# q, k, v and gates in three parts with borders by column group, sigmoid by tanh, and modulation work moved around the first attention

## The chip, the cores and the metric

The kernel runs on one core of one Trainium2 chip. The metric is the device time of one execution in microseconds, the median of several runs. TensorE (PE) multiplies, with its weight loads (PEld) beside it; VectorE (DVE), ScalarE (ACT) and GpSimd (POOL) do the rest; SyncE's queue (SP) issues all transfers.

## What is computed

A trunk of two layers over 256 tokens of width 2048, all in float32. Cut to what matters here:

```python
c_act = silu(c)
for l in range(2):
    mod = c_act @ ada_w[l] + ada_b[l]                   # 6 x 2048
    sh_a, sc_a, gt_a, sh_m, sc_m, gt_m = split(mod, 6)
    h = rmsnorm(x, norm_mix[l]) * (1 + sc_a) + sh_a
    qa, ka, va, qb, kb, vb, ga, gb = split_cols(h @ w_in[l])
    ya = window_attention(rotary(rmsnorm(qa)), rotary(rmsnorm(ka)), va, sink) @ w_proj_a[l]
    yb = neighbourhood_attention(rmsnorm(qb), rmsnorm(kb), vb, bias) @ w_proj_b[l]
    x = x + gt_a * ((sigmoid(ga) * ya + sigmoid(gb) * yb) @ w_out[l])
    h = rmsnorm(x, norm_ffn[l]) * (1 + sc_m) + sh_m
    g, v = split(depthwise_conv(h @ w_up[l]), 2)
    x = x + gt_m * ((silu(g) * v) @ w_down[l])
```

## The kernel before

**Weights.** The host lays all weight matrices out as a stream of 128x128 blocks in the order in which they are used (`block_stream`). A *unit* is 16 blocks, 1 MiB, one transfer (`w<-in_ws`, L255) into one of the four buffers of the pool `raw`. ACT casts each half of a unit to a rounded high part (L264), DVE subtracts it from the weight for the low part (L265); both lie in one of the four buffers `hl`. PE multiplies with three products (high by high, low by high, high by low). `features` has weights as the stationary side and 256 tokens as the moving one, 3 matmuls of 256 columns a block (L273 to L275). `tokens`, used for q, k, v, has the activations stationary and four blocks, 512 columns, moving (L331 to L333), for two halves of the tokens. A unit is 48 matmuls of 256 columns or 24 of 512. A layer is 232 units.

**Modulation.** `ada` makes `mod` in 96 steps a layer: each loads 1 MiB (`aw<-in_aw`, L195) into a buffer of the same pool `raw`, and one DVE instruction (L196) multiplies it by silu(c) and sums it. Steps 0 to 31 of layer 0 give shift and scale of the first norm; `ada_and_h` makes chunk kc of the modulated input h (16 chunks of 128 features; `normed`, L403 on DVE, L406 on ACT, L407 on DVE) after its two steps.

**Order of the work.** Each time the stream has used up a unit, `tick` runs: background jobs in `Paced` advance by their rate (steps per unit), and `plan(l, u)` makes modulation steps until their number lies on the line between the corners (unit, steps) of `ADA_PLAN_0` or `ADA_PLAN_1`. In layer 0 the job that makes h has the rate `FIRST_RATE`. From this the framework places each instruction in its engine's queue, which runs in order.

**Layer 0, stage by stage (unit numbers are those of the stream).** The input projection runs over the 2048 inputs in four parts of 2, 4, 5 and 5 chunks of h (`K_PARTS_0`), so that it can begin before h is complete. In each part come nine groups of 512 columns of q, k, v (`QKV_GROUPS`) and 16 chunks of gate A; a part begins when all its chunks of h are in the program. The borders lie at units 6.5, 19.5 and 35.75, the end at 52. In the first part ACT copies the sums out (L751, L787); in the later ones DVE adds them to what is there (L753, L782). In the last part `qk_rows` normalises q and k (L483 to L509; the power of -0.5 on POOL, L378) and turns them on PE (L516). The job `attention` starts after the third group of the last part with rate `ATT`, one new head at most a step, eight heads A and then eight heads B: scores (L528), row maximum (L532), exp (L540), scaling by the reciprocal (L548), transposes (L553), product with v (L559), between the matmuls of the stream. Gate A gets its sigmoid in the last part (L785). Then come the projection of A times its gate (L796, units 52 to 60), gate B with its sigmoid (L810, units 60 to 76), the projection of B times gate B plus ya, split into high and low (L822 to L824), the output projection and the feed-forward network.

**Layer 1** has its h complete before the projection, which is one part there; eight gate chunks are made first from the not yet normalised input (`bare_gate`, L663).

```python
for pi, part in enumerate(parts):
    if l == 0 and pi > 0:
        while done[0] < 2 * (part[-1] + 1):
            next(job0)
    last = pi == len(parts) - 1
    for g in range(len(QKV_GROUPS)):
        pss = st.tokens(h, part)
```

Of the kernel before, what the change touches and what calls it, by code (L numbers as in the profile page):

```python
# [9 lines left out]
F32 = mybir.dt.float32  # L10
F32R = mybir.dt.float32r
AF = mybir.ActivationFunctionType
ALU = mybir.AluOpType
AX = mybir.AxisListType

P = 128
L = 2
D = 2048
S = 256
KC = D // P  # L20
# [12 lines left out]
QKV_GROUPS = [1024, 0, 512, 2560, 3584, 1536, 3072, 4096, 2048]  # L33
GATE_A, GATE_B = 4608, 6656
# [2 lines left out]
FF_GROUPS = [list(range(sum(FF_SIZES[:i]), sum(FF_SIZES[: i + 1]))) for i in range(3)]  # L37


K_PARTS_0 = [2, 4, 5, 5]  # L40
K_PARTS = [[range(sum(K_PARTS_0[:i]), sum(K_PARTS_0[: i + 1])) for i in range(len(K_PARTS_0))], [range(KC)]]

FIRST_TURN = 3
OUT_TURNS = [range(0, FIRST_TURN)] + [[mo] for mo in range(FIRST_TURN, KC)]

ADA_PLAN_0 = [(38, 32), (58, 48), (76, 66), (84, 70), (98, 80), (108, 80), (231, 143)]
ADA_PLAN_1 = [(8, 143), (76, 166), (84, 168), (99, 176), (108, 176), (128, 184), (142, 192)]

FIRST_RATE = 0.65
ENDING = 15  # L50
FIRST = 0

# [18 lines left out]
def block_stream(l):  # L71

    seq = []
    bare = BARE[0] if l else 0
    if l:
        for kc in range(KC):
            seq += [("w_in", kc, GATE_A // P + mo) for mo in range(SIDE)]
        for mo in range(SIDE, bare):
            seq += [("w_in", kc, GATE_A // P + mo) for kc in range(KC)]
    for part in K_PARTS[l]:  # L80
        for g in QKV_GROUPS:
            for kc in part:
                seq += [("w_in", kc, g // P + j) for j in range(4)]
        for mo in range(bare, KC):
            seq += [("w_in", kc, GATE_A // P + mo) for kc in part]
    for mo in range(KC):
        seq += [("w_proj_a", kc, mo) for kc in range(HA)]
    for mo in range(KC):
        seq += [("w_in", kc, GATE_B // P + mo) for kc in range(KC)]
    for mo in range(KC):  # L90
        seq += [("w_proj_b", kc, mo) for kc in range(HB)]
    for mos in OUT_TURNS:
        seq += [("w_out", kc, mo) for kc in range(KC) for mo in mos]
    for gi, chunks in enumerate(FF_GROUPS):
        cols = [c + h * FC for c in chunks for h in range(2)]
        if gi == 0:
            for kc in range(KC):
                seq += [("w_up", kc, m) for m in cols[:SIDE]]
            cols = cols[SIDE:]
        for m in cols:  # L100
            seq += [("w_up", kc, m) for kc in range(KC)]
        for mos in OUT_TURNS:
            seq += [("w_down", kc, mo) for kc in chunks for mo in mos]
    return seq
# [11 lines left out]
def encoder(ctx: ExitStack, tc: tile.TileContext, a: dict, out: bass.AP):  # L116
    nc = tc.nc
# [14 lines left out]
    at = pool("at", 2)  # L132
# [40 lines left out]
    def led(name):  # L173

        t = hp.tile([P, KC * 2 * S + OFF], F32R, name=name, tag="h")
        at = [0] + [OFF + 2 * S * k for k in range(1, KC)]
        return [t[:, i : i + 2 * S].rearrange("p (a s) -> p a s", a=2) for i in at]
# [6 lines left out]
    mods, amods, nrms, done = {}, {}, {}, {0: 0, 1: 0}  # L184
# [63 lines left out]
    bg = Paced()  # L248
# [86 lines left out]
                    self.tick()  # L335
            return pss

    def split(dst, src):
        nc.scalar.copy(dst[:, 0], src)
        nc.vector.tensor_tensor(out=dst[:, 1], in0=src, in1=dst[:, 0].bitcast(F32), op=ALU.subtract)  # L340

    def warm(n):

# [73 lines left out]
    class Bare:  # L417
# [47 lines left out]
        def at(self):  # L465
            return {SQUARES_AT: self.squares, ROOTS_AT: self.roots}

        def level(self, ps):

            z = ev.tile([P, S], F32, name="lev", tag="z")  # L470
            sh = sm.tile([P, 3], F32, name="lsh", tag="lsh")
            nc.scalar.activation(out=sh[:, 1:], in_=ps[:, S : S + 2], func=AF.Copy, accum_out=sh[:, :1])
            nc.vector.tensor_tensor(out=z[:], in0=ps[:, :S], in1=self.rbs[:], op=ALU.mult)
            return z, sh

# [103 lines left out]
    def plan(l, u):  # L579

        corners = (ADA_PLAN_0, ADA_PLAN_1)[l]
        for (u0, n0), (u1, n1) in zip(corners, corners[1:]):
# [33 lines left out]
    ps = ax.tile([P, 2], F32, name="ss_in", tag="ss", bufs=1)  # L616
# [28 lines left out]
    for l in range(L):  # L645
        st = Stream(l) if l == 0 else nxt
        mod = mods.get(l)
        if l == 0:
            h = led("h0_0")
            job0 = ada_and_h(first_h(h))  # L650
            while done[0] < 2 * len(K_PARTS[0][0]):
                next(job0)
            mod = mods[0]
            bg.add(job0, FIRST_RATE)

        ya = place("o", 16, F32, f"ya{l}")
        if l:


            def bare_gate(mo):  # L660
                def evac(ps):
                    z, sh = bare.level(ps)
                    nc.scalar.activation(out=ya[:, mo], in_=z[:], func=AF.Sigmoid, bias=sh[:, :1])  # L663

                return evac

            st.features(bare.chunks, [bare_gate(mo) for mo in range(SIDE)], at=bare.at())
            for mo in range(SIDE, BARE[0]):
                st.features(bare.chunks, [bare_gate(mo)])
            bg.finish(bare.steps)  # L670
            h = bare.h
# [61 lines left out]
                next(job)  # L733

        hs = h
        parts = K_PARTS[l]
        for pi, part in enumerate(parts):
            if l == 0 and pi > 0:
                while done[0] < 2 * (part[-1] + 1):
                    next(job0)  # L740
            last = pi == len(parts) - 1
            for g in range(len(QKV_GROUPS)):
                pss = st.tokens(h, part)
                if pi == 0 and g == 0:
                    gains, sink, cw, rots = small(l)
                dst = packs[g // 3][:, 4 * (g % 3) : 4 * (g % 3) + 4]
                rows = dst.rearrange("p (t a) s -> p t (a s)", t=2)
                if not last or pi > 0:
                    for t, ps in enumerate(pss):
                        if pi == 0:  # L750
                            nc.scalar.copy(rows[:, t], ps[:])  # L751
                        else:
                            nc.vector.tensor_tensor(out=rows[:, t], in0=ps[:], in1=rows[:, t], op=ALU.add)  # L753
                    pss = [rows[:, t] for t in range(2)]
                if not last:
                    continue

                def have(g=g):
                    ready[0] = g + 1

                vcol = {0: GA * HEAD, 4: 0, 7: 0}.get(g)
                if vcol is not None and pi == 0:
                    for t in range(2):
                        nc.scalar.copy(rows[:, t, vcol:], pss[t][:, vcol:])
                if g == 0:
                    qk_rows(pss, GA, rots[1], gains[:, 1:2], kTa, have)
                elif g < 3:
                    qk_rows(pss, 4, rots[0], gains[:, 0:1], dst, have)
                elif vcol is None:
                    qk_rows(pss, 4, None, gains[:, 3:4] if g in (3, 6) else gains[:, 2:3], dst, have)  # L770
                else:
                    have()
                if g == 2:
                    bg.add(job, ATT[l])


            for mo in range(BARE[0] if l else 0, KC):

                def gate_a(ps):
                    src = ps  # L780
                    if pi > 0:
                        nc.vector.tensor_tensor(out=ya[:, mo], in0=ps, in1=ya[:, mo], op=ALU.add)  # L782
                        src = ya[:, mo]
                    if last:
                        nc.scalar.activation(out=ya[:, mo], in_=src, func=AF.Sigmoid)  # L785
                    elif pi == 0:
                        nc.scalar.copy(ya[:, mo], ps)  # L787

                st.features([hs[k] for k in part], [gate_a])


        attended(HA)
        for mo in range(KC):

            def proj_a(ps):
                nc.vector.tensor_tensor(out=ya[:, mo], in0=ps, in1=ya[:, mo], op=ALU.mult)  # L796

            st.features(oA, [proj_a])
        bg.pace(job, ATT_B[l])
        gb = []  # L800
# [6 lines left out]

        def gate_b(mo):
            def evac(ps):
                nc.scalar.activation(out=gb[mo], in_=ps, func=AF.Sigmoid)  # L810

            return evac

# [3 lines left out]
        merged = led(f"merged{l}")  # L817
        for mo in range(KC):

            def merge(ps):  # L820
                z = ev.tile([P, S], F32, name="m", tag="z")
                nc.vector.tensor_tensor(out=z[:], in0=ps, in1=gb[mo], op=ALU.mult)  # L822
                nc.vector.tensor_tensor(out=z[:], in0=z[:], in1=ya[:, mo], op=ALU.add)
                split(merged[mo], z[:])  # L824

            st.features(oB, [merge])

# [6 lines left out]
        bare = Bare(l, 1, sums)  # L834
# [27 lines left out]
        for gi, chunks in enumerate(FF_GROUPS):  # L862
# [34 lines left out]
            for cs in sets:  # L897
                fns = [lambda p, e=e, c=c: e(p, c) for c in cs for e in (g_evac, v_evac)]
                src = bare.chunks if gi == 0 and cs[0] < BARE[1] // 2 else bare.h
# [36 lines left out]
        if l < L - 1:  # L936
            bare = over
# [75 lines left out]
```

## Time and profile before

| | |
|---|---|
| Time, median of 3 runs | 2703.92 us (2703.27 to 2705.94) |
| The profiled execution | 2704.2 us, span 2702.4 us, granted clock 0.996 |
| PE busy | 2660.9 us, 98% of the span |
| DVE busy | 2099.4 us, 78% |
| ACT busy | 1411.0 us, 52% |
| Transfers | 700.38 MB, mean 259 GB/s |
| DVE, weights' low parts (L265) | 928 of 1222 ns |
| DVE, modulation steps (L196) | 192 of 2348 ns |
| ACT, weights' high parts (L264) | 928 of 1049 ns |
| ACT, table loads | 29 of 1283 ns |

The profile is of one execution. A busy PE need not run at its pace: matmuls are pipelined and a late one counts as busy for longer, so the number of matmuls in a stretch says more than the share. Durations of neighbours on DVE and ACT overlap by some 0.09 us: a duration is the mean of one instruction, and the chain of waits shows what each adds.

### The profile page before, as it was taken

To read this page: it belongs to the slowest core of one execution; us is meant where nothing else is said; L and a number is where in the kernel's file an instruction comes from. 1 tells how busy PE (TensorE), PEld (TensorE's weight loads), DVE (VectorE), ACT (ScalarE), POOL (GpSimd) and SP (SyncE) were. 2 spreads that over 40 slices of the span, in tenths; PEclk is the share of its full clock that TensorE was granted. 3 is DMA by queue.
4 is the path that set the end of the run, shared out by engine and by line. 5 is a ranking of instruction groups with operands and counts; after the bars stand their busy time and mean duration, and the time that the engine had idled before them with its cause. 6 is when DMAs were issued, how large, how long until landed. Compare 5 with 4: busy or idle time off the path is not lost.

```text
span 2702.4 us, 50217 instructions
## 1 busy us (share of the span) xinstructions
PE 2660.9 (98%) x21088; PEld 2565.8 (95%) x21088; DVE 2099.4 (78%) x2941; ACT 1411.0 (52%) x2081; POOL 35.1 (1%) x24
## 2 busy tenths in 40 slices
PE   7899999999999999999999999999999999999999
PEld 5688799999999999999998889999999999999999
DVE  6998987897987888788886666658879866655664
ACT  5344684455754455345564556544565445543553
POOL 0000100000000000000000000000000000000000
PEclk9899999999999999999999999999999999999999
DMA  8887578987688888878766656666757775555554
GB/s 319 329 340 272 218 288 313 356 309 265 235 296 297 291 293 286 296 290 297 291 217 250 241 209 231 233 237 254 292 184 283 285 265 197 188 200 190 190 200 142
DMA packets 101892, 700.38 MB, mean 259 GB/s; under 512 B 12705, under 2 KB 15009, under 8 KB 17697
## 3 DMA queue, kind: packets, MB, share of 16 engines
q1 hardware_dynamic: 101666, 697.17, 70.7%
q8 instruction: 165, 2.70, 0.4%
q14 instruction: 61, 0.50, 0.0%
HBM read 695.03 MB, written 2.10 MB: 258 GB/s over the span
## 4 chain that ended last, share of the span: by engine, by line
PE 91%; DVE 4%; DMA 1%; ACT 1%; POOL 1%; issue 1%; SPq 0%; POOLq 0%; ACTq 0%; DVEq 0%
PE ps L273 26%; PE ps L275 25%; PE ps L274 25%; PE ps_t L332 4%; PE ps_t L333 4%; PE ps_t L331 4%; DVE aw L196 1%; DVE hl L265 1%; PE po L559 1%; PE sc L528 1%; DMA aw<-in_aw 1%; POOL qrs L378 1%; PE tp L553 0%; ACT hl L264 0%; DVE qn L492 0%
## 5 line engine op out<-in xcount | busy, mean ns | idle before, releaser
L265 DVE TENSOR_TENSOR hl<-w,hl 128x1024 fp32r<-128x1024 f32 x928 | 1130.2, 1222 | 362.5 <-ACT hl L264 360.9
L264 ACT CAST hl<-w 128x1024 fp32r<-128x1024 f32 x928 | 971.1, 1049 | 771.9 <-PE ps L275 487.1
L273 PE MATMUL ps<-h,hl 128*128 128x256 f32 x3328 | 925.1, 278 | 0.0
L275 PE MATMUL ps<-h,hl 128*128 128x256 f32 x3328 | 923.6, 278 | 0.9 <-DVE hl L265 0.9
L274 PE MATMUL ps<-h,hl 128*128 128x256 f32 x3328 | 921.9, 277 | 0.0
L275 PEld LDWEIGHTS ps<-h,hl 128*128 128x128 f32 x3328 | 625.4, 188 | 1.5 <-DVE hl L265 1.3
L273 PEld LDWEIGHTS ps<-h,hl 128*128 128x128 f32 x3328 | 625.9, 188 | 0.5
L274 PEld LDWEIGHTS ps<-h,hl 128*128 128x128 f32 x3328 | 625.3, 188 | 0.4
L196 DVE CUSTOM_DVE_ANT_0 aw<-aw,cact,ab 128x2048 f32<-128x2048 f32 x192 | 450.8, 2348 | 62.8 <-DMA aw<-in_aw 62.0
L331 PE MATMUL ps_t<-hl,h 128*128 128x512 f32 x576 | 227.4, 399 | 7.9 <-ACT hl L264 7.3
L332 PE MATMUL ps_t<-hl,h 128*128 128x512 f32 x576 | 228.4, 397 | 5.2 <-DVE hl L265 5.2
L333 PE MATMUL ps_t<-hl,h 128*128 128x512 f32 x576 | 228.1, 396 | 0.9 <-DVE h L407 0.9
L858 DVE SCALAR_TENSOR_TENSOR u<-ps,cw,u 128x255 f32<-128x255 f32 x304 | 146.2, 481 | 68.0 <-ACT u L856 64.0
L856 ACT ACTIVATE u<-ps,cw 128x256 f32<-128x256 f32 x152 | 85.7, 564 | 185.6 <-PE ps L275 185.4
L275 PE MATMUL ps<-merged,hl 128*128 128x256 f32 x512 | 142.1, 278 | 0.0
L274 PE MATMUL ps<-merged,hl 128*128 128x256 f32 x512 | 141.8, 277 | 0.0
L273 PE MATMUL ps<-merged,hl 128*128 128x256 f32 x512 | 141.8, 278 | 0.0
L274 PE MATMUL ps<-act_o,hl 128*128 128x256 f32 x512 | 141.6, 277 | 0.0
L275 PE MATMUL ps<-act_o,hl 128*128 128x256 f32 x512 | 141.6, 276 | 0.0
L273 PE MATMUL ps<-act_o,hl 128*128 128x256 f32 x512 | 141.4, 277 | 0.0
L331 PEld LDWEIGHTS ps_t<-hl,h 128*128 128x128 f32 x576 | 109.5, 190 | 31.9 <-ACT hl L264 8.4
L332 PEld LDWEIGHTS ps_t<-hl,h 128*128 128x128 f32 x576 | 109.8, 191 | 30.9 <-DVE hl L265 8.2
(209 smaller groups left out, 4574.1 us busy)
## 6 DMA issues: line engine op xcount, KB each, us to landing
w<-in_ws SPq DMA_DIRECT2D x464, 1024.0 KB, 4.9
aw<-in_aw SPq DMA_DIRECT2D x192, 1024.0 KB, 5.7
bias<-in_bias SPq DMA_DIRECT2D x16, 256.0 KB, 4.5
x<-in_xT SPq DMA_DIRECT2D x4, 512.0 KB, 5.4
out<-x SPq DMA_DIRECT2D x16, 128.0 KB, 2.3
cw<-in_cw SPq DMA_DIRECT2D x2, 176.0 KB, 4.5
maskA<-in_maskA SPq DMA_DIRECT2D x1, 256.0 KB, 5.3
ab<-in_ab SPq DMA_DIRECT2D x2, 48.0 KB, 6.1
```

Of the source, the lines that this page charges most:

```text
L196: nc.vector.tensor_tensor_reduce(out=raw[:], in0=raw[:], in1=cact[:], scale=1.0, scalar=ab[:, i : i + 1], op0=ALU.mult, op1=ALU.add, accum ...
L264: nc.scalar.copy(hl[:, 0], r)
L265: nc.vector.tensor_tensor(out=hl[:, 1], in0=r, in1=hl[:, 0].bitcast(F32), op=ALU.subtract)
L273: nc.tensor.matmul(out, hi, act[0], start=first, stop=False)
L274: nc.tensor.matmul(ps[:, :S], hi, act[1], start=False, stop=False)
L275: nc.tensor.matmul(out, lo, act[0], start=False, stop=last)
L331: nc.tensor.matmul(ps[:], xh, hi, start=kc == kcs[0], stop=False)
L332: nc.tensor.matmul(ps[:], xh, lo, start=False, stop=False)
L333: nc.tensor.matmul(ps[:], xl, hi, start=False, stop=kc == kcs[-1])
L378: nc.gpsimd.tensor_tensor(out=dst, in0=src, in1=mhalf[:, :k], op=ALU.pow)
L856: nc.scalar.activation(out=u, in_=ps, func=AF.Identity, scale=w[:, 1:2], bias=w[:, 3:4])
L858: nc.vector.scalar_tensor_tensor(out=u[:, to], in0=ps[:, of], scalar=w[:, j : j + 1], in1=u[:, to], op0=ALU.mult, op1=ALU.add)
```

## The change

It has three parts. The parts of layer 0's projection are three instead of four, and each column group has its own border: the first part takes 2 chunks of h for the first three groups, 3 for two, 4 for four and 6 for the gates, the second goes on to 8 to 12 and 13, the third to the end. The first part ends with unit 13, the second with unit 35, the third with unit 52. The rate of the job that makes h is 1.1, 0.85 and 0.7 in the parts instead of 0.65. Sigmoid(z) is computed as (1 + tanh(z/2)) / 2: ACT makes the tanh, the 1 + is added where the gate is multiplied, and the factor 1/2 is applied where the merged rows are split. The plan of modulation steps in layer 0 has other corners: from unit 30 to 40 it goes from 32 to 40, to 49 at unit 61 and to 67 at unit 76; from unit 84 on it is as before.

```diff
-K_PARTS_0 = [2, 4, 5, 5]
-K_PARTS = [[range(sum(K_PARTS_0[:i]), sum(K_PARTS_0[: i + 1])) for i in range(len(K_PARTS_0))], [range(KC)]]
+K_ENDS = [
+    [([2, 2, 2, 3, 3, 4, 4, 4, 4], 6), ([8, 8, 9, 10, 10, 11, 10, 10, 12], 13), ([KC] * 9, KC)],
+    [([KC] * 9, KC)],
+]
+def k_parts(l):
+    parts, at, gat = [], [0] * len(QKV_GROUPS), 0
+    for ends, gend in K_ENDS[l]:
+        parts.append(([range(a, e) for a, e in zip(at, ends)], range(gat, gend)))
+        at, gat = ends, gend
+    return parts
...
-ADA_PLAN_0 = [(38, 32), (58, 48), (76, 66), (84, 70), (98, 80), (108, 80), (231, 143)]
+ADA_PLAN_0 = [(30, 32), (40, 40), (61, 49), (76, 67), (84, 70), (98, 80), (108, 80), (231, 143)]
...
-FIRST_RATE = 0.65
+FIRST_RATE = [1.1, 0.85, 0.7]
...
-    def split(dst, src):
-        nc.scalar.copy(dst[:, 0], src)
-        nc.vector.tensor_tensor(out=dst[:, 1], in0=src, in1=dst[:, 0].bitcast(F32), op=ALU.subtract)
+    def split(dst, src, scale=None):
+        if scale is None:
+            nc.scalar.copy(dst[:, 0], src)
+            nc.vector.tensor_tensor(out=dst[:, 1], in0=src, in1=dst[:, 0].bitcast(F32), op=ALU.subtract)
+            return
+        nc.scalar.activation(out=dst[:, 0], in_=src, func=AF.Identity, scale=scale)
+        nc.vector.scalar_tensor_tensor(
+            out=dst[:, 1], in0=src, scalar=scale, in1=dst[:, 0].bitcast(F32), op0=ALU.mult, op1=ALU.subtract
+        )
+    def half_tanh(dst, src, **kw):
+        nc.scalar.activation(out=dst, in_=src, func=AF.Tanh, scale=0.5, **kw)
+    def gated(dst, half, src):
+        nc.vector.scalar_tensor_tensor(out=dst, in0=half, scalar=1.0, in1=src, op0=ALU.add, op1=ALU.mult)
...
-                    nc.scalar.activation(out=ya[:, mo], in_=z[:], func=AF.Sigmoid, bias=sh[:, :1])
+                    half_tanh(ya[:, mo], z[:], bias=sh[:, :1])
...
-        parts = K_PARTS[l]
-        for pi, part in enumerate(parts):
-            if l == 0 and pi > 0:
-                while done[0] < 2 * (part[-1] + 1):
-                    next(job0)
+        parts = k_parts(l)
+        def have_h(part):
+            while l == 0 and done[0] < 2 * part.stop:
+                next(job0)
+        for pi, (groups, gates) in enumerate(parts):
             last = pi == len(parts) - 1
-            for g in range(len(QKV_GROUPS)):
+            if l == 0:
+                bg.pace(job0, FIRST_RATE[pi])
+            for g, part in enumerate(groups):
+                have_h(part)
                 pss = st.tokens(h, part)
...
+            have_h(gates)
...
-                        nc.scalar.activation(out=ya[:, mo], in_=src, func=AF.Sigmoid)
+                        half_tanh(ya[:, mo], src)
...
-                nc.vector.tensor_tensor(out=ya[:, mo], in0=ps, in1=ya[:, mo], op=ALU.mult)
+                gated(ya[:, mo], ya[:, mo], ps)
...
-                nc.scalar.activation(out=gb[mo], in_=ps, func=AF.Sigmoid)
+                half_tanh(gb[mo], ps)
...
-                nc.vector.tensor_tensor(out=z[:], in0=ps, in1=gb[mo], op=ALU.mult)
+                gated(z[:], gb[mo], ps)
                 nc.vector.tensor_tensor(out=z[:], in0=z[:], in1=ya[:, mo], op=ALU.add)
-                split(merged[mo], z[:])
+                split(merged[mo], z[:], 0.5)
```

More of the change, by code (lines that the diff above doesn't have):

```diff
@@ L79, in block_stream @@
             seq += [("w_in", kc, GATE_A // P + mo) for kc in range(KC)]
-    for part in K_PARTS[l]:
-        for g in QKV_GROUPS:
+    for parts, gates in k_parts(l):
+        for g, part in zip(QKV_GROUPS, parts):
             for kc in part:
@@ L84, in block_stream @@
         for mo in range(bare, KC):
-            seq += [("w_in", kc, GATE_A // P + mo) for kc in part]
+            seq += [("w_in", kc, GATE_A // P + mo) for kc in gates]
     for mo in range(KC):
@@ L466, in at, with level @@
             return {SQUARES_AT: self.squares, ROOTS_AT: self.roots}
-        def level(self, ps):
+        def level(self, ps, scale=1.0):
             z = ev.tile([P, S], F32, name="lev", tag="z")
             sh = sm.tile([P, 3], F32, name="lsh", tag="lsh")
-            nc.scalar.activation(out=sh[:, 1:], in_=ps[:, S : S + 2], func=AF.Copy, accum_out=sh[:, :1])
+            nc.scalar.activation(out=sh[:, 1:], in_=ps[:, S : S + 2], func=AF.Copy, scale=scale, accum_out=sh[:, :1])
             nc.vector.tensor_tensor(out=z[:], in0=ps[:, :S], in1=self.rbs[:], op=ALU.mult)
@@ L650, in encoder @@
             job0 = ada_and_h(first_h(h))
-            while done[0] < 2 * len(K_PARTS[0][0]):
+            while done[0] < 2 * K_ENDS[0][0][0][0]:
                 next(job0)
             mod = mods[0]
-            bg.add(job0, FIRST_RATE)
+            bg.add(job0, FIRST_RATE[0])
         ya = place("o", 16, F32, f"ya{l}")
@@ L661, in evac @@
                 def evac(ps):
-                    z, sh = bare.level(ps)
-                    nc.scalar.activation(out=ya[:, mo], in_=z[:], func=AF.Sigmoid, bias=sh[:, :1])
+                    z, sh = bare.level(ps, 0.5)
+                    half_tanh(ya[:, mo], z[:], bias=sh[:, :1])
                 return evac
@@ L784, in gate_a @@
                     if last:
-                        nc.scalar.activation(out=ya[:, mo], in_=src, func=AF.Sigmoid)
+                        half_tanh(ya[:, mo], src)
                     elif pi == 0:
                         nc.scalar.copy(ya[:, mo], ps)
-                st.features([hs[k] for k in part], [gate_a])
+                st.features([hs[k] for k in gates], [gate_a])
         attended(HA)
```

## The prediction

> **What bounds the kernel now.** I read the page first, then the windows by stage, the chain of waits around the first break, the transfers in the crowded stretch and the groups.
>
> ```profile
> PE 2660.9 (98%) x21088; PEld 2565.8 (95%) x21088; DVE 2099.4 (78%) x2941; ACT 1411.0 (52%) x2081; POOL 35.1 (1%) x24
> ...
> PEclk9899999999999999999999999999999999999999
> ```
>
> PE is the bound, so only stretches in which PE runs below its own pace can give anything. The pace is read from the windows.
>
> ```profile
> 30.00:64.00 34.00, 34.00 (x175) 28.65 (x175) 24.54 (x32) 24.74 (x42) 0.00 (x0) 0.96 0.78 291
> 64.00:92.00 28.00, 18.38 (x76) 14.05 (x75) 25.65 (x33) 9.90 (x16) 0.00 (x0) 0.76 0.94 354
> ...
> 117.00:239.00 122.00, 121.11 (x723) 107.93 (x722) 117.37 (x153) 50.28 (x53) 0.00 (x0) 1.00 0.87 325
> ...
> 267.00:413.00 146.00, 138.30 (x882) 122.44 (x881) 130.35 (x261) 108.53 (x210) 13.58 (x6) 0.99 0.68 251
> ...
> 437.00:491.00 54.00, 54.00 (x477) 54.00 (x476) 39.96 (x39) 21.55 (x29) 0.00 (x0) 1.00 0.93 340
> 491.00:521.00 30.00, 29.10 (x249) 28.67 (x249) 25.56 (x26) 13.07 (x18) 0.00 (x0) 1.00 0.96 365
> ```
>
> Columns: window, length, then PE, PEld, DVE, ACT, POOL busy with counts, granted clock, DMA share, GB/s. From 437 to 491 PE did 477 matmuls of 256 columns in 54 us, 0.113 us each; a unit of weights (1 MiB, 16 blocks, 48 such matmuls or 24 of 512 columns) is 5.45 us. Counting matmuls in the timeline, unit 6 starts at 64.3, 8 at 89.4, 13 at 116.6, 35 at 239.3, 40 at 267.3, 57 at 413.1, 58 at 420.4, 76 at 520.7. Against 5.45 a unit that is 14.2 us lost over units 6 and 7, 3.5 over units 8 to 39, and 2.2 over units 58 to 75. Units 40 to 56 need 92.7, and the A and B heads' matmuls and transposes about 40 (216 and 109 ns each), of 145.8: 13 lost. Layer 1's attention (1524 to 1830) keeps PE busy throughout, with some 3 us of small gaps. So some 30 us of layer 0 is within reach.
>
> ```profile
> 62.32 1.23 DVE hl L265
> 63.54 2.27 DVE aw L196
> 66.01 2.26 DVE aw L196
> 68.28 0.40 DVE ht L403
> 68.68 2.26 DVE aw L196
> 70.95 0.40 DVE h L407
> ...
> 74.60 2.26 DVE aw L196
> ```
>
> This chain of 55 to 100 shows the first break: the second part wants h 2 to 5 at once, and DVE makes aw 7 to 11 back to back while PE waits and its clock falls to 0.76.
>
> ```profile
> DMA packets 3419, 24.89 MB, mean 356 GB/s; under 512 B 385, under 2 KB 385, under 8 KB 385
> ```
>
> That is the transfers of 460 to 530 at 95% and more busy: 1 MiB in 2.95 us. From 64 to 80 it was 370 GB/s, 2.83 us.
>
> **Part by part: the borders by group.** Nothing before the first unit changes. In the changed program's order on DVE, aw 4 stands ahead of unit 1's splits and fills an idle 3.3 us there (DVE waits for the cast from 31.7 to 35.0); aw 5, aw 6 and h 2 stand ahead of unit 2's. With the 2.26, 1.13 and 0.40 of the chain, unit 2 starts at about 43.7 instead of 41.6: 2 us worse. From there one h is wanted about every 1.5 to 3 units, and 1.1 aw come with each unit. DVE to unit 13: 14 aw at 2.34 (32.8), 24 splits at 1.135 (27.2), 7 h at 0.9 (6.3), then aw 18 and a split (3.5) with one idle us, from 31.7: 102.5 at the earliest. Transfers: 11.4 MiB lie there at 34; by unit 13 some 25 more are wanted (w to 13, aw to 18, a part of the next), after about 1 us without a free buffer: 35 + 25 x 2.87 = 106.8 at a rate between the two rows (105.8 to 108.8). I take 107: the transfer is the later. Gain **9.5 us** (2.8 if a MiB takes 3.15, the mean of 460 to 500; 14 at DVE's limit).
>
> Units 13 to 40: one pass of additions is gone, 18 pack additions at 0.60 and 16 gate additions at 0.35 of DVE (54 and 48 become 36 and 32), 16.4 us; against it, 21 aw fall in these units instead of 17, 9.4 us. DVE was 96% busy from 117 to 239 and falls little; the border at unit 19.5, with 1.2 us of waiting, goes, and no later h is closer than a unit to its use in the changed order. A unit takes 5.5 rather than 5.58: **2.3 us** (between -1 and 3.5, all that is lost there).
>
> **The attention.** Between units 40 and 57 the plan asks for 7.3 aw instead of 13.6: 6.3 x 2.34 = 14.7 us less of 130 of DVE.
>
> ```profile
> L540 ACT ACT_TABLE_LOAD x12 | 15.4, 1283 | 0.2
> L785 ACT ACT_TABLE_LOAD x9 | 11.5, 1283 | 0.1
> ```
>
> Of 29 table loads the changed program keeps 6: its tanh between two exps has none. Of the 23 gone, ten lie in these units (13 of 108 us of ACT), one in unit 60, twelve in layer 1. A sigmoid between heads costs ACT 1.28 each way in front of the softmax chain that PE waits for (transposes for L548, packs' transposes for L492). In the trace a load has 17 ns before it and the next operation follows at once. The Trainium skill (ScalarE: Activation LUTs, What ACT_TABLE_LOAD costs) adds a drain of 1.38 to each switch; no run here shows one, and by it ACT would save 61 us in all instead of 29.5, still off PE's path. The heads start 1.25 units later in the new order (first scores in unit 43 instead of 42) and end in unit 55 instead of 57, so they stand closer. The 13 us lost fall from nothing (if they are latency) to 13 (if queues); the heads' crowding could cost 4. Half is nearest to two engines at 89% and 74% going to 79% and 66%: **7 us**.
>
> The other exchanges are nothing: sigmoid to tanh is one ACTIVATE of 410 for another; `gated` and the scaled split turn 128x256 TENSOR_TENSOR of 420 into SCALAR_TENSOR_TENSOR of 480 (L407), 96 times 60 ns, 5.8 us of DVE, and 32 CASTs of 405 into ACTIVATE of about 410, in stages where PE is the bound and DVE under 85%. Without that cover it would be the 5.8. Layer 1's loads go from stretches without PE gaps to speak of: 0, at most 3.
>
> **What is given back.** The aw taken out of the attention come in units 61 to 76: 18 in 15 units instead of 18 in 18. Each issues 1 MiB on SP's queue, between the units' weights, and both share the four `raw` buffers. Before, 36 MiB at 2.95 make 106.2 against 100.3 measured: the buffers that stood full at the start absorbed 5.9, and PE lost 2.2 (491 to 521 shows it). After, 33 MiB in 15 units make 97.4 against 81.8 of PE: 15.6 short, 5.9 absorbed, 9.7 lost, so **7.5 us** worse than before. At 2.87 it would be 4.9, at 3.15 14, and nothing at the 435 GB/s of the fastest slices. The Trainium skill (HBM Reference, Specifications) gives a core streaming alone about 425 GB/s and about 358 as its share; the 356 here agrees with the second figure. With the first, an estimate from that page is 2.47 us a MiB and nothing lost here. From unit 76 the plans agree.
>
> **Sum.** The profiled execution took 2704.2 (span 2702.4 and 1.8 around it), 0.3 over the median. 2704.2 - 9.5 - 2.3 - 7 + 7.5 = 2692.9; with the 0.3, **2693**.
>
> **Rivals.** *Transfers are free*: the two crowded stretches run at the 430 GB/s that single slices show. The start falls to DVE's 102.5 (14), gate B loses nothing and gets its 2.2 back: 2704 - 14 - 2.3 - 7 - 2.2 = 2678. Against it: a 95% busy stretch moved 356. Chance 0.17. The Trainium skill's 425 GB/s (HBM Reference, Specifications) would make this case. *The attention stays*: its gaps are the latency of scores, max, exp, transpose, which neither aw nor loads lengthen: 2700 (2696 to 2705). For it: no single wait of PE there is over 2.0 us. Chance 0.20. *Slower*: w and aw together do not get through at 1.1 and 1.2 aw a unit. At 3.15 us a MiB the start gains 2.8; units 13 to 28 with 1.85 MiB each take 5.83 and lose 3.8; gate B costs 14 more; the attention gives 7: 2704 - 2.8 + 3.8 + 14 - 7 = 2712. It decides from about 3.08 us a MiB (340 GB/s) on. For it: 437 to 491 ran at 340 with 93% busy. Chance 0.13. *It does not do what it says* is out for the loads (the program has 6) and for the order of h (as read); 0.02 for anything else. The forecast keeps 0.48.
>
> **The numbers.** A measurement of this kernel tells 0.2%, 5.4 us, from no change: faster is under 2698.5, slower over 2709.3. Forecast: 0.45 faster, 0.03 same. Free transfers: 0.17 faster. Attention: 0.06 faster, 0.13 same, 0.01 slower. Slow transfers: 0.01 same, 0.12 slower. The rest: 0.01 same, 0.01 slower. Together 0.68, 0.18, 0.14. The range leaves out the slow transfers and the far end of the free ones: 2678 to 2706.
>
> **What would show it.** Right: no break between 64 and 92, granted clock 1.0 there, unit 13 near 107, unit 35 near 229; DVE under 82% and ACT under 68% over units 40 to 56, and these units about 7 us shorter; 480 to 521 of before with PE gaps whose last wait is a landing of w or aw, about 10 us in all. Wrong: unit 13 not before 113; the attention as long as before; or no gaps in units 66 to 76.

## The result and the profile after

The changed kernel is slower: a median of 2710.74 us over 10 runs (2707.58 to 2718.62) against 2704.93 over 10 runs of the kernel before (2700.64 to 2709.96). The ratio is 1.0025, 95% interval 1.0016 to 1.0034. The profiled execution took 2709.15 us, span 2707.4, granted clock 0.998. The forecast was 2693.

The page of the kernel after, engines and clock:

```profile
PE 2662.9 (98%) x21088; PEld 2562.5 (95%) x21088; DVE 2088.8 (77%) x2907; ACT 1380.0 (51%) x2058; POOL 33.0 (1%) x24
...
PEclk9999999999999999999999999999999999999999
```

ACT lost 31 us and 23 instructions, and the clock's second slice reads 9 instead of 8. Those parts went as forecast, and yet the time rose. The windows of the kernel after, in the stretches shown of before (window, length, PE, PEld, DVE, ACT, POOL busy with counts, clock, DMA share, GB/s), with the start, 26 to 116, added:

```profile
26.00:116.00 90.00, 80.47 (x457) 68.42 (x457) 75.97 (x93) 44.73 (x69) 0.00 (x0) 0.96 0.86 331
...
30.00:64.00 34.00, 30.53 (x115) 22.88 (x114) 26.54 (x35) 16.17 (x23) 0.00 (x0) 0.95 0.80 301
64.00:92.00 28.00, 26.26 (x170) 23.10 (x169) 25.21 (x30) 15.57 (x24) 0.00 (x0) 1.00 0.89 362
117.00:239.00 122.00, 118.64 (x660) 100.67 (x661) 112.01 (x130) 47.63 (x51) 0.00 (x0) 1.00 0.88 330
267.00:413.00 146.00, 138.68 (x820) 120.52 (x821) 118.21 (x265) 99.58 (x213) 12.71 (x6) 0.99 0.58 210
437.00:491.00 54.00, 54.00 (x477) 54.00 (x477) 46.51 (x45) 21.26 (x28) 0.00 (x0) 1.00 0.95 375
491.00:521.00 30.00, 29.38 (x255) 29.03 (x254) 24.98 (x24) 12.02 (x16) 0.00 (x0) 1.00 0.96 371
```

The break between 64 and 92 is gone (clock 1.00 instead of 0.76). But 30 to 64 has 115 matmuls instead of 175, and 117 to 239 has 660 instead of 723. No engine and no queue is full over 26 to 116: DVE is busy for 84%, the transfers for 86%. This is the line to keep in mind for all that follows. The kernel before had moved no more over the same stretch, with a DMA share of 0.85:

```profile
26.00:116.00 90.00, 78.15 (x361) 63.63 (x360) 78.10 (x99) 44.99 (x69) 0.00 (x0) 0.91 0.85 318
```

Starts of units, by counted matmuls in the two timelines (here and below "units 13 to 29" is the time from the start of unit 13 to the start of unit 30; the expectations call the stretch from the start of 40 to the start of 57 "units 40 to 57"):

| unit | before | after | after is later by |
|---|---|---|---|
| 2 | 41.6 | 45.5 | 3.9 |
| 6 | 64.3 | 72.4 | 8.1 |
| 8 | 89.4 | 83.8 | -5.6 |
| 13 | 116.6 | 116.1 | -0.5 |
| 30 | 211.2 | 215.8 | 4.6 |
| 39 | 261.7 | 264.8 | 3.1 |
| 61 | 436.9 | 440.2 | 3.3 |
| 84 | 564.5 | 570.0 | 5.5 |

From unit 84 to the end the two agree within 0.5 us. So by stage the time changed by -0.5 us to unit 13, +3.5 to unit 39, +0.3 to unit 61, +2.2 to unit 84 and -0.5 behind it: the +5.0 between the two profiled executions. The border is set at unit 39, where the prediction had 40, because the attention's first stall falls into unit 40 before (10.2 us for this unit) and into unit 39 after (9.9). Counted from unit 40, the stretch ahead of it lost 7.8 and the attention won 4.0. What the finer borders win by unit 8 is given back by unit 13: units 8 to 12 took 27.2 before, PE's own pace, and 32.3 after.

The chain of waits after, from 44 to 110, shows why (the row `issue` covers the time in which ACT makes h; ACT's own row from the timeline stands below):

```profile
48.07 2.26 DVE aw L209
50.57 0.50 DVE ht L431
51.12 0.39 issue
51.51 1.04 ACT hl L277
52.58 1.24 DVE hl L278
53.86 0.50 PE ps_t L345
...
91.08 2.26 DVE aw L209
93.35 2.27 DVE aw L209
95.86 0.50 DVE ht L431
96.40 0.39 issue
96.79 1.04 ACT hl L277
97.87 0.58 PE ps L286
```

```profile
51.09 0.51 ACT L434 ACTIVATE h<-ht,mod 128x256 fp32r<-128x256 f32 x1 [2.26 <-DVE ht L431]
```

PE waits for a unit's low part (L278). That waits for ACT's cast (L277), which stands in ACT's queue behind h (L434), and h waits for `ht` (L431), which stands on DVE behind one or two modulation steps (L209). It is the chain of before with one or two steps in front instead of five in a row, but it now recurs: at 48, 62, 84 and 91 in this stretch.

### The profile page after: what moved, and what is told of

Its sections match the earlier page's. It is cut to its first block, busy times and chain, and to the rows that moved or that the text cites. A ratio compares the mean times of both kernels' runs of the same rounds, so it can differ in the third digit from the quotient of the medians.

```text
span 2707.4 us, 50160 instructions
## 1 busy us (share of the span) xinstructions
PE 2662.9 (98%) x21088; PEld 2562.5 (95%) x21088; DVE 2088.8 (77%) x2907; ACT 1380.0 (51%) x2058; POOL 33.0 (1%) x24
## 4 chain that ended last, share of the span: by engine, by line
PE 90%; DVE 6%; ACT 1%; issue 1%; DMA 1%; POOL 1%; SPq 0%; ACTq 0%; POOLq 0%; DVEq 0%
PE ps L286 26%; PE ps L288 26%; PE ps L287 26%; PE ps_t L345 3%; PE ps_t L346 3%; PE ps_t L344 3%; DVE hl L278 2%; DVE aw L209 2%; PE po L587 1%; PE sc L556 1%; ACT hl L277 1%; POOL qrs L406 1%; DMA aw<-in_aw 1%; PE tp L581 1%; PE qtp L544 0%
## 5 line engine op out<-in xcount | busy, mean ns | idle before, releaser
L278 DVE TENSOR_TENSOR hl<-w,hl 128x1024 fp32r<-128x1024 f32 x928 | 1129.8, 1222 | 379.5 <-ACT hl L277 378.2
L277 ACT CAST hl<-w 128x1024 fp32r<-128x1024 f32 x928 | 969.3, 1049 | 755.2 <-PE ps L288 507.8
L209 DVE CUSTOM_DVE_ANT_0 aw<-aw,cact,ab 128x2048 f32<-128x2048 f32 x192 | 450.7, 2348 | 54.1 <-DMA aw<-in_aw 53.2
```

What stands on the lines that cost most here:

```text
L209: nc.vector.tensor_tensor_reduce(out=raw[:], in0=raw[:], in1=cact[:], scale=1.0, scalar=ab[:, i : i + 1], op0=ALU.mult, op1=ALU.add, accum ...
L277: nc.scalar.copy(hl[:, 0], r)
L278: nc.vector.tensor_tensor(out=hl[:, 1], in0=r, in1=hl[:, 0].bitcast(F32), op=ALU.subtract)
```

## The experiments: one part of the change at a time

**Borders and rates alone.** The changed kernel with the plan of before, and the sigmoid of before at every gate.

```diff
-ADA_PLAN_0 = [(30, 32), (40, 40), (61, 49), (76, 67), (84, 70), (98, 80), (108, 80), (231, 143)]
+ADA_PLAN_0 = [(38, 32), (58, 48), (76, 66), (84, 70), (98, 80), (108, 80), (231, 143)]
...
-                        half_tanh(ya[:, mo], src)
+                        nc.scalar.activation(out=ya[:, mo], in_=src, func=AF.Sigmoid)
...
```

> The borders and the rates of h alone: sigmoid and the plan of modulation steps as before. In the changed kernel unit 13 began at 116.1 us (before 116.6) and unit 39 at 264.8 (before 261.7). Theory 1 (the start gained nothing because each h puts DVE and ACT in one chain): unit 13 again near 116, unit 39 at 261 to 265, the time 0 to 3 us over before. Theory 2 (the start is as good as before and the loss over units 13 to 39 is the plan's 8 early modulation steps in units 30 to 40): unit 39 near 260, the time 1 to 4 us under before.

2705.53 against 2705.05, ratio 1.0004 (0.9995 to 1.0012): nothing. Unit 13 at 116.3, unit 30 at 216.0. The start's missing gain lies here.

**Tanh alone.** The changed kernel with the four uniform parts, the rate 0.65 and the plan of before.

```diff
-    [([2, 2, 2, 3, 3, 4, 4, 4, 4], 6), ([8, 8, 9, 10, 10, 11, 10, 10, 12], 13), ([KC] * 9, KC)],
+    [([e] * 9, e) for e in (2, 6, 11, KC)],
...
-FIRST_RATE = [1.1, 0.85, 0.7]
+FIRST_RATE = [0.65] * 4
```

> Tanh, gated and the scaled split alone, borders and plan as before. ACT loses 23 of 29 table loads. Theory 1 (the attention's PE gaps are latency, and the loads lie beside other work): within 2 us of before, units 40 to 57 in 145 us as before. Theory 2 (the loads stand in front of the softmax chain): 3 to 7 us faster, units 40 to 57 in 139 to 142.

2704.09 against 2705.05, 0.9997 (0.9988 to 1.0006). Units 40 to 56 took 149.1 instead of 145.8: 23 fewer table loads, ten of them in these units, gave no time.

**The plan alone.** The kernel before with the new corners.

```diff
-ADA_PLAN_0 = [(38, 32), (58, 48), (76, 66), (84, 70), (98, 80), (108, 80), (231, 143)]
+ADA_PLAN_0 = [(30, 32), (40, 40), (61, 49), (76, 67), (84, 70), (98, 80), (108, 80), (231, 143)]
```

> The plan of modulation steps alone; h still made at 0.65 a unit, so that the corner at unit 30 pulls some steps of h earlier. Theory 1 (less DVE work in the attention frees nothing, and the steps in units 61 to 76 cost PE about 4 us in waits for transfers): 2 to 6 us slower. Theory 2 (the attention gains from it): units 40 to 57 at least 4 us shorter and the time 0 to 5 us faster.

2715.21 against 2705.05, 1.0037 (1.0024 to 1.0049). A part of this isn't in the changed kernel: with the slow rate of before, the corner (30, 32) draws steps 28 to 31 in one burst between the weights of units 29 and 30, and units 30 to 32 take 22.0 instead of 16.8. In its waits from 211 to 233 PE stands for one low part:

```profile
PE ps_t L332 <- DVE hl L265: 3.6, 1, 3.6
```

Further on, units 39 to 60 took 2.5 us longer than before and units 61 to 79 2.3.

**Borders, rates and tanh, with the old plan.** As the first, but with the tanh kept.

```diff
-ADA_PLAN_0 = [(30, 32), (40, 40), (61, 49), (76, 67), (84, 70), (98, 80), (108, 80), (231, 143)]
+ADA_PLAN_0 = [(38, 32), (58, 48), (76, 66), (84, 70), (98, 80), (108, 80), (231, 143)]
```

> The changed kernel with the old plan of modulation steps. Borders alone and tanh alone were each within 1 us of before, the plan alone 10 us slower. Theory 1 (in the changed kernel the plan costs the whole loss, in units 39 to 41 and 61 to 78): 2703 to 2706 us, 5 under the changed kernel, unit 84 at 564 to 566. Theory 2 (borders and tanh hinder each other in the attention, where tanh alone was 9 us late at unit 55 and made it up): 2708 to 2711.

2707.59 against 2704.11, 1.0010 (0.9996 to 1.0023). With the plan added (the whole change) it is 1.0025: the plan costs some 0.15%, 4 us, though the intervals overlap and so do not settle it.

## The experiments: what paces the start

**h on DVE.** The sum for h's high part moves from ACT to DVE, which takes the crossing between the engines out of the chain and puts DVE work in.

```diff
-            nc.scalar.activation(out=h[kc][:, 0], in_=t[:], func=AF.Identity, bias=sh)
+            if l == 0 and w == 0:
+                nc.vector.tensor_scalar(out=h[kc][:, 0], in0=t[:], scalar1=sh, scalar2=None, op0=ALU.add)
+            else:
+                nc.scalar.activation(out=h[kc][:, 0], in_=t[:], func=AF.Identity, bias=sh)
```

> The changed kernel, but the high part of layer 0's first h is rounded by DVE instead of ACT, so that ACT's queue holds weight casts and copies alone there, and DVE no longer waits for ACT within an h. DVE gets 16 more instructions of about 0.4 us. Theory 1 (the chain modulation step, ht, ACT's h, ACT's cast, DVE's split holds the start): unit 13 at 108 to 112 instead of 116, the time 4 to 8 us under the changed kernel. Theory 2 (transfers and the four raw buffers hold it): unit 13 within 1.5 us of 116, the time within 2 us of the changed kernel.

2719.10 against 2705.05, 1.0057 (1.0043 to 1.0070). Unit 13 at 122.0 (5.9 later than after), unit 30 at 222.0 (6.2 later). Neither theory had a loss. Taking this crossing out gained nothing, and more work on DVE cost time although DVE is 16% idle there: from 44 to 116 there are seven such sums of 0.36 us, 2.5 in all, and DVE waits 10.1 us for ACT's casts of the weights instead of 7.1.

**Cheap modulation steps on DVE** and, apart from it, **small transfers for them**. The first makes DVE work on an eighth of each of the 32 steps' elements and loads them whole; the second loads an eighth of them and lets DVE read that eighth seven times over, in 2.08 us a step instead of 2.35. Both leave out part of the modulation's sums.

```diff
+            c = 256 if l == 0 and n < 2 * KC else D
-                out=raw[:], in0=raw[:], in1=cact[:], scale=1.0, scalar=ab[:, i : i + 1],
+                out=raw[:, :c], in0=raw[:, :c], in1=cact[:, :c], scale=1.0, scalar=ab[:, i : i + 1],
```

```diff
-            nc.sync.dma_start(raw[:], a["aw"][l, n])
+            if l == 0 and n < 2 * KC:
+                nc.sync.dma_start(raw[:, :256], a["aw"][l, n][:, :256])
...
```

> The changed kernel with layer 0's first 32 modulation steps summed over 256 of their 2048 columns on DVE (so the modulation is not the reference's); their transfers are whole. Each step costs DVE some 0.5 us instead of 2.35. Theory 1 (DVE's work paces the start; the run with h on DVE lost 16 times 0.4 us by unit 30, just what it added): unit 13 at 100 to 106 instead of 116, unit 30 at 195 to 203 instead of 216, and the rest as before. Theory 2 (transfers through four buffers pace it): unit 13 not before 112, unit 30 not before 211.

> The changed kernel with an eighth of the transfer of layer 0's first 32 modulation steps (256 of 2048 columns; DVE reads them seven times over, so the modulation is not the reference's). DVE's step costs about 2.1 us instead of 2.35. Theory 1 (DVE paces the start): unit 13 at 112 to 115, only the 0.25 us of 18 steps less. Theory 2 (transfers): unit 13 at 102 to 108, unit 30 before 203.

One run each, beside 2704.11 of before: 2704.34 and 2692.28. Unit 13 came at 109.2 with cheap DVE and at 101.6 with small transfers, unit 30 at 206.3 and 194.5. The windows of the two, cheap DVE first:

```profile
26.00:116.00 90.00, 83.59 (x481) 70.54 (x481) 50.36 (x95) 46.18 (x70) 0.00 (x0) 1.00 0.91 362
```

```profile
26.00:116.00 90.00, 89.93 (x534) 80.17 (x535) 86.16 (x120) 53.28 (x79) 0.02 (x1) 1.00 0.63 223
116.00:239.00 123.00, 123.00 (x706) 108.66 (x705) 111.14 (x131) 49.85 (x52) 0.00 (x0) 1.00 0.74 269
```

With the steps' transfers small, DVE is busy for 86.16 of 90 us and PE has hardly a gap from 26 to 239: DVE alone allows it. With DVE cheap, the transfers move 362 GB/s instead of 331. Each floor of the prediction is nearly reached when the other cost is taken away: 109.2 for 106.8 with cheap DVE, and 101.6 for 102.5 with small transfers. The second is no clean test of DVE's floor, since 14 steps at 0.26 us less are worth 3.7 us and PE runs at its own pace there. With both in place unit 13 comes at 116.1, not at the later of the two. In the kernel after, from 44 to 116, SyncE's queue waits for these:

```profile
SPq L268 <- DVE hl L278: 24.3, 7, 4.4
SPq L268 <- DVE mod L209: 11.4, 3, 5.4
SPq L208 <- DVE amod L216: 10.4, 5, 2.1
SPq L208 <- DVE mod L209: 8.2, 4, 2.6
SPq L208 <- DVE hl L278: 7.9, 4, 4.2
```

Weights (L268) and modulation rows (L208) share the ring, which is refilled in the order in which DVE empties it. While DVE is held by a step, by `ht` or by ACT's cast, no buffer comes free, and the queue of transfers runs dry now and then (14% of the window); while a transfer is late, DVE stands. So the two times add in part. This is a reading of the waits; the runs with one cost taken away, with more work on DVE and with fewer buffers all agree with it.

**Three buffers in the ring.**

```diff
-    rawp = pool("raw", 4)
+    rawp = pool("raw", 3)
```

> The changed kernel with three buffers for weights and modulation tensors instead of four. Theory 1 (the transfers are slow at the start because a buffer comes free too late to keep the queue full, not because the memory gives no more): the DMA share from 26 to 116 falls from 0.86 to 0.65 to 0.75, unit 13 at 125 to 140. Theory 2 (the memory's rate is the limit and the buffers suffice): unit 13 within 4 us of 116.

One run: 2762.74. Unit 13 at 123.0, 6.9 us later than with four, and just under the 125 to 140 expected; the DMA share fell to 0.83, not to 0.65 to 0.75. That is 47.0 over the kernel before on its chip. The ring's depth matters, but a missing buffer costs less at the start than over the rest of layer 0 (unit 84 comes 23.3 later than after). A fifth buffer wasn't tried.

**Lower rates.** Borders as in the first experiment, other rates.

```diff
-FIRST_RATE = [1.1, 0.85, 0.7]
+FIRST_RATE = [0.9, 0.7, 0.65]      # the second: [0.75, 0.6, 0.65]
```

> Borders alone (sigmoid and the plan as before), with the rates 0.9, 0.7, 0.65 instead of 1.1, 0.85, 0.7: unit 13's weights are queued behind 17 modulation steps instead of 19, unit 29's behind 28 instead of 32. Theory 1 (transfers through four buffers pace units 2 to 30, some 3.2 us a MiB): unit 13 at 109 to 112 instead of 116, unit 30 at 204 to 208 instead of 216, the time 5 to 9 us under before if the attention is as long as with borders alone. Theory 2 (the chain of each h paces it, whatever lies in the queue): unit 13 within 2 us of 116, the time within 2 us of before.

> As the run with 0.9, with rates 0.75, 0.6, 0.65, so that more steps of h are made at the border that wants them and not ahead of it. Unit 13's weights stand behind 16 modulation steps. Theory 1: unit 13 at 107 to 112, unit 30 at 202 to 207, the time 5 to 10 us under before. Theory 2: as with borders alone, unit 13 near 116.

2702.61 and 2706.75 against 2715.72 on their chip: 0.9956 (0.9938 to 0.9974) and 0.9973 (0.9957 to 0.9990). Unit 13 at 111.0 and 111.3, unit 30 at 204.5 and 204.3. The fast rates put 19 modulation steps ahead of unit 13's weights and 32 ahead of unit 29's; at 0.9 it is 17 and 28, at 0.75 16 and 27. The four steps that are no longer ahead at unit 29 make 4 x 2.87 = 11.5 us of transfers at the prediction's rate and 12.7 at the 331 GB/s of the changed kernel; unit 30 came 11.5 earlier than in the first experiment (204.5 for 216.0). The fifth step fewer, at 0.75, gave no more: with 0.9 units 13 to 29 already take 93.4, 5.5 each, close to PE's own pace of 5.45. None of these steps was wanted so early: units 13, 30, 61 and 84 all came earlier without them (84 at 552.4 for 564.9).

## The experiments: the attention, gate B, and a better kernel

**Cheap steps in the attention.** The kernel before; DVE works on an eighth of steps 32 to 47 (it leaves out part of their sums).

```diff
+            c = 256 if l == 0 and 2 * KC <= n < 3 * KC else D
-                out=raw[:], in0=raw[:], in1=cact[:], scale=1.0, scalar=ab[:, i : i + 1],
+                out=raw[:, :c], in0=raw[:, :c], in1=cact[:, :c], scale=1.0, scalar=ab[:, i : i + 1],
```

> The kernel before, with modulation steps 32 to 47 of layer 0 (units 38 to 58) summed over 256 of 2048 columns on DVE (so the modulation is not the reference's); transfers whole. DVE has some 30 us less to do during the attention, more than the new plan takes from it. Theory 1 (its PE gaps are the latency of the chains of each head and of each column group): units 40 to 57 in 143 to 146 us (146 before). Theory 2 (queueing on DVE): 133 to 140.

One run: 2701.75; units 40 to 56 took 148.3, not fewer than the 145.8 of before. DVE was busy for 105.30 us of 265 to 413 there, some 25 less than before, and it gave nothing.

**Heads further apart**, once in the kernel before and once with the borders, the sigmoid and the plan of the first experiment and the rates 0.9, 0.7, 0.65.

```diff
-ATT = [1.288, 0.4]
+ATT = [1.0, 0.4]
```

> The kernel before, with the attention job at 1.0 steps a unit instead of 1.288, so that a head's transposes come 5.45 us of PE work after its scores instead of 4.2. Theory 1 (PE's gaps in the attention are each head's latency from scores to the scaled rows, DVE and ACT work not being what holds it: 30 us less of DVE and ten table loads less changed nothing): the waits of transposes for ACT's p fall from 2.6 us to under 1, the waits for the column groups' qn (3.6) stay, the time 1 to 4 us under before. Theory 2 (the waits are queueing, and the job is merely spread): within 1 us of before or slower.

> Borders with rates 0.9, 0.7, 0.65 (sigmoid, old plan) and the attention job at 1.0 a unit. Theory 1: 1 to 4 us under the run with these rates alone, 13 to 16 under before. Theory 2: the same as that run, 10 to 13 under before.

2704.81 against 2705.06, 0.9998 (0.9988 to 1.0007), and 2701.69, 0.9984 (0.9975 to 0.9993). In the first, PE's waits from 250 to 425 include

```profile
PE tp L553 <- ACT p L548: 1.4, 3, 0.9
```

where the kernel before has 2.6 for this wait, and no time comes of it (units 39 to 60: 174.9 for 175.2). With the lower rates it makes these units worse, 177.5 against 171.8.

**Gate B's steps spread out.** The changed kernel without the corner at 76.

```diff
-ADA_PLAN_0 = [(30, 32), (40, 40), (61, 49), (76, 67), (84, 70), (98, 80), (108, 80), (231, 143)]
+ADA_PLAN_0 = [(30, 32), (40, 40), (61, 49), (84, 70), (98, 80), (108, 80), (231, 143)]
```

> The changed kernel with the corner at unit 76 taken out of the plan: steps 49 to 70 lie on one line from unit 61 to 84, 0.91 a unit instead of 1.2 and then 0.375. Theory 1 (1.2 a unit is more than the transfers carry, and costs 2 to 4 us in units 72 to 78): units 61 to 84 in 125.5 to 127 instead of 129.8, the time 2 to 4 us under the changed kernel. Theory 2 (what the plan costs lies in units 39 to 61): units 61 to 84 within 1 us of 129.8.

2721.67 against 2715.72, 1.0023 (1.0006 to 1.0039), no better than the change as it is. Units 61 to 77 took 92.8 instead of 97.0, and units 78 to 83 took 37.4 instead of 32.8: the loss is only displaced.

**Lower rates with tanh**, the old plan kept; and **the same with a gentler new plan**.

```diff
-FIRST_RATE = [1.1, 0.85, 0.7]
+FIRST_RATE = [0.9, 0.7, 0.65]
-ADA_PLAN_0 = [(30, 32), (40, 40), (61, 49), (76, 67), (84, 70), (98, 80), (108, 80), (231, 143)]
+ADA_PLAN_0 = [(38, 32), (58, 48), (76, 66), (84, 70), (98, 80), (108, 80), (231, 143)]  # the first
+ADA_PLAN_0 = [(36, 32), (40, 35), (61, 49), (76, 67), (84, 70), (98, 80), (108, 80), (231, 143)]  # the second
```

> The changed kernel with the rates 0.9, 0.7, 0.65 and the old plan: borders and tanh. Theory 1 (with the start mended the change is good but for its plan; tanh gives and takes nothing): 10 to 13 us under before, as with these rates and sigmoid. Theory 2 (tanh takes 2 to 4 us in the attention, where the heads end later with it): 6 to 9 under before.

> All three parts of the change with the rates 0.9, 0.7, 0.65; the plan's first corners are at (36, 32) and (40, 35), so that it no longer pulls the last steps of h forward, then as in the change 49 at unit 61 and 67 at unit 76. Theory 1 (the early steps of h by the rates were the larger loss and the plan's crowding of units 61 to 76 the smaller): 5 to 9 us under before, 3 to 5 over the run with rates and tanh and the old plan, and that between units 61 and 80. Theory 2 (the plan is the larger loss): within 3 us of before.

**2694.81** against 2705.06, 0.9959 (0.9946 to 0.9972), and 2698.09, 0.9970 (0.9958 to 0.9982). The first is 10 us under before and, by the medians of two sets of runs, 16 under the changed kernel, so it beats both. Unit 13 comes at 112.8, 30 at 206.1, 61 at 429.2, 84 at 554.9, 9.6 us ahead of before. (Its profiled execution, 2701.95 us, was the longest of its runs; the excess lies behind unit 84.) The new plan wins 2.1 us in units 39 to 60 (170.6 for 172.7) and loses 6.8 in units 61 to 79 (110.6 for 103.8). The windows in gate B of the first and of the second:

```profile
482.00:532.00 50.00, 50.00 (x441) 50.00 (x441) 43.54 (x57) 23.56 (x33) 0.00 (x0) 1.00 0.92 344
```

```profile
482.00:532.00 50.00, 47.70 (x397) 46.88 (x396) 43.02 (x55) 21.97 (x30) 0.00 (x0) 0.97 0.92 354
```

With the old plan PE is full at its pace, 441 matmuls in 50 us; with the new one 44 are missing.

## Why the prediction was wrong, and where it was right

The sum had -9.5, -2.3, -7 and +7.5, together -11.3; the two profiled executions differ by +5.0. The 16.3 between them are what the start (9.0), the units from 13 up to the attention (5.8) and the attention (7.3) gained too little, less what gate B lost too little (5.3) and the 0.5 won behind unit 84. (With the prediction's border at unit 40 the second is 10.1 and the third 3.0.)

**The failing step: "I take 107: the transfer is the later."** Two floors were worked out, DVE's 102.5 and the transfers' 106.8, and the later one was taken. The experiments with one cost taken away come near both floors (109.2 and 101.6), but the rule for joining them is wrong: unit 13 came at 116.1, since in a ring of four buffers that DVE empties in order each waits for the other. Over 26 to 116 the transfers moved 331 GB/s at a share of 0.86. That is 3.17 us for a MiB on the clock, against the 2.87 of the sum, which was read in stretches with the queue 95% and more busy. With 3.17 the prediction's own sum gives 35 + 25 x 3.17 = 114.3, near the 116.1. The 318 GB/s of the kernel before over the same stretch was there to be read.

**Units 13 to 40: the term of 5.5 us a unit was mis-sized.** Units 13 to 29 took 99.7, 5.86 each, where the kernel before took 94.6. Again the transfers set the pace: 1.85 MiB come with each unit there, at 331 GB/s 5.86 us, and with small transfers these units took 92.9. With cheap DVE they still took 97.2, so DVE's work alone isn't what keeps the queue from being full here; what else does is not shown. Units 30 to 38 gave 1.5 back (49.0 for 50.5). That the steps were ahead of need was not weighed at all. The prediction counted the 21 steps instead of 17 as DVE time, 9.4 us, under savings of 16.4; what they did to the transfers was asked only in the rival "Slower". Lower rates alone recover it, and they turn the whole into a gain: from 1.0010 (0.9996 to 1.0023) with the fast rates to 0.9959 (0.9946 to 0.9972), the rest the same.

**The attention: the 7 us was taken from a loss that none of the runs recovered.** "13 lost" was a stretch less an estimate of its work. PE's named waits from 265 to 420 sum to 7.5 in the kernel before, these two the largest sums,

```profile
PE tp L553 <- ACT p L548: 2.6, 3, 1.2
PE qtp L516 <- DVE qss L377: 2.0, 1, 2.0
```

and after the change they are

```profile
PE qtp L544 <- DVE qn L537: 4.9, 3, 2.1
PE tp L581 <- ACT p L576: 3.8, 4, 1.3
```

8.7 us, although from 267 to 413 DVE has 12 us less and ACT 9 less. Units 39 to 60 took 175.5 for 175.2, and units 40 to 56 143.6 for 145.8. Fewer modulation steps, fewer table loads, 25 us less of DVE and more room between the heads each gave nothing; the rival "the attention stays" was right in this. Its reason, latency, is not shown: what holds the stage stays open. The new plan, added to the tanh and the lower rates, shortened units 39 to 60 by 2.1 us; added to the borders with tanh and fast rates it lengthened them by 2.5 (173.0 to 175.5), as it did alone. With one trace of each, that is no gain to speak of. The Trainium skill (ScalarE: Activation LUTs, What ACT_TABLE_LOAD costs) adds a drain of 1.38 us to each switch; 23 switches fewer changed the time by a ratio of 0.9997 (0.9988 to 1.0006), so with or without a drain they lay off PE's path.

**Gate B: the direction was right, 7.5 was 2.2.** The transfers in this stretch, 460 to 530 of the kernel after:

```profile
DMA packets 3663, 26.67 MB, mean 381 GB/s; under 512 B 413, under 2 KB 413, under 8 KB 413
```

381 GB/s where before moved 356. At 2.75 us a MiB, 33 MiB take 90.8, 9.0 over PE's 81.8; less the 5.9 absorbed, 3.1 is lost and 0.9 more than before, nearer to the 2.2 measured. The 2.2 that the kernel before lost there is itself not the rule. In seven of the ten traces with the old corners units 61 to 79 took 103.8, PE's own pace; before took 105.7. In the six with the corner (76, 67) and four buffers they took 107.9 (the changed kernel) to 110.6. Against PE's pace the plan thus lost 4.1 in the changed kernel, where 9.7 was forecast, and 6.8 with the lower rates. The rate of a crowded stretch is the uncertain quantity here. The Trainium skill (HBM Reference, Specifications) has 358 GB/s as a core's share and about 425 for one alone; the stretches shown here with a DMA share of 0.92 to 0.97 moved 340 to 381, below the larger figure each time and on both sides of the smaller.

**The rival "Slower"** has the total, 2712 for 2710.7, and two of its terms: unit 13 hardly earlier, and 5.83 us a unit from 13 on for the 5.86 measured. That weights and modulation rows together do not get through was right. It took a rate of 340 GB/s or less from a stretch that was 93% busy; the runs show 331 over 26 to 239 with transfers that stand idle for 11 to 14% of the time. Its total is partly luck, because two errors cancel: gate B lost 2.2 instead of 14, the attention won nothing instead of 7.

**Right:** the break of 64 to 92 went and the clock rose there; unit 2 came later (3.9 us, forecast 2); six table loads remain, of which this line and another have two each and two lines have one each:

```profile
L568 ACT ACT_TABLE_LOAD x2 | 2.6, 1283 | 0.0
```

The tanh, the `gated` products and the scaled split cost nothing, and behind unit 84 nothing changed. Of the conditions named for "wrong", two came true: unit 13 not before 113, and the attention as long as before (175.5 for 175.2 from unit 39; from unit 40 it was 2 us shorter, not 7).

## What to carry to other kernels

Where one ring of buffers feeds several consumers and one engine empties it in order, don't simply take the later of the transfer's and the engine's floor: here, 4 us apart, they added in part, and the sign was that both were busy for 80 to 90% and neither was full. Take the rate of the transfers from the stretch itself in the kernel before, or say why it should rise; a stretch with a full queue gave a higher one here. Background work has a rate at which the borders want it, and the steps ahead of that cost about their transfers' time here, as long as transfers paced the stage. Before a stage's missing time is entered as a gain, add up the waits that the trace names there: an estimate of the work subtracted from the stretch isn't a wait.

## What was unexpected in the hardware

The transfer rate in a crowded stretch isn't a constant of the program: with much the same mix of 1 MiB transfers, 460 to 530 moved 356 GB/s in one kernel and 381 in the other at a DMA share of 0.96 and 0.97, and 437 to 491 moved 340 and 375 at 0.93 and 0.95. What sets it wasn't found. Of these windows the granted clock was lowest where PE stood longest: before, 0.76 in 64 to 92 with 76 matmuls; after, 1.00 there with 170 and 0.95 in 30 to 64 with 115. But not every gap brought a dip: with cheap DVE PE was busy for 83.59 of 90 us from 26 to 116 at a clock of 1.00, the same as with small transfers, where it was busy for 89.93.
